# Down projection with weight sums made in HBM by transfers, seven products for sixteen groups

## The chip, the cores and the metric

One of the eight cores of a Trainium2 chip runs the kernel. The metric is the device time of one execution in microseconds. Engines: PE multiplies (TensorE), DVE and ACT (VectorE and ScalarE) work on vectors, POOL is GpSimd, SP only issues transfers. Matrix products of float32 data are made here in three passes: an operand is split into a high part (`hi`, type float32r) and the rest (`lo`), and high x high, low x high and high x low are added up in PSUM.

## The reference

A block of a language model on x of 256 rows by 2048, all in float32: normalization, a wide input projection, three kinds of attention, gates, an output projection, and a gated feed-forward part. The down projection at its end is what the change touches:

```python
def reference(x, mem, g_mix, w_in, ...):
    ...
        g = jax.nn.sigmoid(gates.reshape(b, s, N_BRANCH, D_MODEL) + b_gate[l])
        merged = (g[:, :, 0] * (o_fox @ w_br_fox[l])
                  + g[:, :, 1] * (o_sb @ w_br_sb[l])
                  + g[:, :, 2] * (o_mem @ w_br_mem[l]))
        x = x + merged @ w_out[l]

        h2 = rms_norm(x, g_ffn[l])
        u = causal_depthwise_conv(h2 @ w_up[l], conv_w[l], conv_b[l])
        u_gate, u_val = jnp.split(u, 2, axis=-1)
        x = x + (jax.nn.silu(u_gate) * u_val) @ w_down[l]
    return x
```

`w_down` has 5632 rows and 2048 columns.

## The kernel before, in words

The stages follow each other: memory keys and values, attention projections with the heads between them, gates and branch products (`w_in`, `w_br_*`; from about 301 us), output projection (`w_out`, first load at 658.6 us), up projection (`w_up`, first load at 748.4 us) and down projection (`w_down`, first load at 1239.7 us).

**Weights.** Everywhere a weight tile of 128 partitions by 1024 float32 (512 KB) is loaded by SP into a ring of four buffers (tag `raw`, `WBUFS` = 4), ACT casts it to `hi` and DVE subtracts to get `lo` (rings of four each, `SBUFS`). In the stages ahead of the down projection that is `piece` (L135 to L137), in the down projection `load` (L785) and `parts` (L792, L793). A raw buffer is free for the next load when its last reader, mostly the DVE subtraction, is done.

**Background work.** `later` puts a generator in a queue; `tick()`, called once after each weight piece (and twice in each group of the down projection), advances up to two of them by one step. `finish()` ticks until none is left. The order of instructions on an engine is then settled by the framework's scheduler, which takes what is ready by priority; DMAs on one issuing engine start in its order, and `keep_in_program_order` holds an instruction to its place.

**Down projection.** The 44 tiles of rows of `w_down` are taken in 22 groups of two, once for each half of the columns (`nb` = 0, 1; `n0` = 0, 1024). Y and X are four PSUM banks each. A letter of `plans` says how a group is made:

- `e`, function `eight`: eight products of 128x128 by 128x512 (two row tiles of the input, two column pieces, two row tiles of weights), three matmuls each: 24 matmuls, two loads.
- `s`, function `seven`: a scheme of Strassen's kind for the group's 2x2 blocks: seven products, 21 matmuls. It needs sums of weight blocks, B01 and B11 being the second halves of the two raw tiles: T1 = B00 + B01, T3 = B11 + B01 (`t13`), T2 = T1 + B11, T4 = T2 + B10 (`t24`), made on DVE (L828, L829, L832, L833), and sums of the input's blocks, made once for each group by `forms` (L774 to L781) and kept in `sf` for both halves (eight places). `gather` adds Y's banks into the residual after the last `s`.

`forms` is called behind an eight while sevens are left in this half. `sums` gives a DVE scratch tile from a ring of two.

In `plans` before, the first half has 5 sevens and 17 eights, the second 7 and 15. At the end of a half, four adds (L893) and transfers (L894, issued by ACT) bring the result out. No transfer is issued by POOL.

Of the kernel before, what the change touches and what calls it, by code (L numbers as in the profile page):

```python
# [9 lines left out]
F32 = mybir.dt.float32  # L10
F32R = mybir.dt.float32r
AF = mybir.ActivationFunctionType
ALU = mybir.AluOpType
AX = mybir.AxisListType

P = 128
# [16 lines left out]
PIECE = 1024  # L33
# [8 lines left out]
def hybrid_block(  # L42
# [25 lines left out]
    nc = tc.nc  # L68
# [3 lines left out]
    wp = ctx.enter_context(tc.tile_pool(name="wp", bufs=WBUFS))  # L72
# [8 lines left out]
    def bank(name):  # L81
        return pp.tile([P, 512], F32, tag="bank", name=name)
# [14 lines left out]
    def later(gen):  # L97
        waiting.append(gen)

    def tick():  # L100
        while waiting and len(active) < WINDOW:
            active.append([waiting.popleft(), 0])
        for a in list(active):
            if a[1] > 0:
                a[1] -= 1
                continue
            try:
                a[1] = next(a[0]) or 0
            except StopIteration:
                active.remove(a)  # L110
# [7 lines left out]
    def finish():  # L118
        while waiting or active:
            tick()  # L120

    pinned = [True]

# [181 lines left out]
    def block(name, dt=F32):  # L305
        return bp.tile([P, 1024], dt, tag="blk", name=name)
# [4 lines left out]
    def rows_of(b):  # L311
        return b.rearrange("p (t n) -> p t n", t=NT)
# [72 lines left out]
    transposed(memT, memres, gmem, 2, "mT")  # L385
    kv_part(0, 1, wh1[:, 0], wl1[:, 0])
    tick()
    xT = None
    for k in range(1, KT):
# [52 lines left out]

    ps = proj(C_MQ, MEM_W, "mq")
    finish()
    qm = heads_of(block("qm"))
    y = norm_heads(ps, rstd, "mq")
# [164 lines left out]
        later(sb_head(h))  # L611


    mT = [None] * (KT // 2)
    branches = ((w_br_fox, 0, N_FOX, 0), (w_br_mem, N_FOX + N_SB, N_MEM, 2), (w_br_sb, N_FOX, N_SB, 1))

    def merged_T(acc, n):
        yield 2
        for pr in range(2):
            m = block(f"mT_{n}_{pr}", F32R).rearrange("p (j s) -> p j s", j=2)  # L620
            tp = bank(f"mt_{n}_{pr}")
            for j in range(2):
                for t in range(NT):
                    c = (2 * pr + j) * P
                    nc.tensor.transpose(tp[:, j * S + t * P : j * S + (t + 1) * P], acc[:, t, c : c + P], ident)
            for j in range(2):
                split_to(m[:, j], tp[:, j * S : (j + 1) * S])
            mT[2 * n + pr] = m
            yield

    for n in range(4):
        n0 = n * 512
        gate = []
        for b in range(3):
            bg = gp.tile([P, 512], F32, tag="bg", name=f"bg_{n}_{b}")
            nc.sync.dma_start(bg, b_gate[0, b, n0 : n0 + 512].partition_broadcast(P))
            ps = proj(C_GATE + b * D + n0, 512, f"g{n}_{b}")
            g = rows_of(block(f"g_{n}_{b}"))
            for t in range(NT):
                nc.vector.scalar_tensor_tensor(g[:, t], ps[t], rstd[:, t : t + 1], bg, ALU.mult, ALU.add)  # L640
            if n > 0:
                nc.scalar.activation(g, g, AF.Sigmoid)
            gate.append(g)
        if n == 0:
            finish()
            for g in gate:
                nc.scalar.activation(g, g, AF.Sigmoid)
        acc = rows_of(block(f"acc_{n}"))
        for i, (w, k0, nk, b) in enumerate(branches):
            ps = product(lambda k: oT[:, k0 + k], w[0], nk, n0, 512, f"b{n}_{b}")  # L650
            for t in range(NT):
                g = gate[b]
                if i == 0:
                    nc.vector.tensor_tensor(acc[:, t], g[:, t], ps[t], ALU.mult)
                else:
                    nc.vector.tensor_tensor(g[:, t], g[:, t], ps[t], ALU.mult)
                    nc.vector.tensor_tensor(acc[:, t], acc[:, t], g[:, t], ALU.add)
        later(merged_T(acc, n))


    hT = xt_pool.tile([P, KT, 2 * S], F32R, tag="xt", name="hT")
# [67 lines left out]
    for f0 in range(0, FT, 4):  # L729
        for s in range(2):  # L730
            ps = [bank(f"u{f0 + i}_{s}") for i in range(4)]
            c0 = s * D_FF + f0 * P
            for k in range(0, KT, 2):
                hi, lo = piece(upv[:, k : k + 2, c0 : c0 + 512], 2, 512, f"u{f0}_{s}_{k}")
                for j in range(2):
                    first, last = k + j == 0, k + j == KT - 1
# [18 lines left out]
    def sums(name):  # L755

        if not dn:
            uv.close()
            dn.append(ctx.enter_context(tc.tile_pool(name="dn", bufs=2)))
        return dn[0].tile([P, 1024], F32, tag="ts", name=name)  # L760

    ov = out[0].rearrange("(t p) d -> p t d", p=P)
    dv = w_down[0].rearrange("(k p) n -> p k n", p=P)
    FS3, FS1, FS2, FS4 = range(4)
    sf = xt_pool.tile([P, 8, 4, 2, P], F32R, tag="xt", name="sf")

# [16 lines left out]
    def load(k, n0):  # L783
        raw = wp.tile([P, PIECE], F32, tag="raw", name=f"raw_d{n0}_{k}")
        nc.sync.dma_start(raw, dv[:, k, n0 : n0 + PIECE])  # L785
        return raw

    def parts(src, name):
        n = src.shape[1]
        hi = wp.tile([P, PIECE], F32R, tag="hi", bufs=SBUFS, name=f"hi_{name}")  # L790
        lo = wp.tile([P, PIECE], F32R, tag="lo", bufs=SBUFS, name=f"lo_{name}")
        nc.scalar.copy(hi[:, :n], src)  # L792
        nc.vector.tensor_tensor(lo[:, :n], src, hi[:, :n].bitcast(F32), ALU.subtract)  # L793
        return [(hi[:, i : i + 512], lo[:, i : i + 512]) for i in range(0, n, 512)]

    def three(o, ah, al, w, first=False, last=False):
        nc.tensor.matmul(o, lhsT=ah, rhs=w[0], start=first, stop=False)  # L797
        nc.tensor.matmul(o, lhsT=al, rhs=w[0], start=False, stop=False)  # L798
        nc.tensor.matmul(o, lhsT=ah, rhs=w[1], start=False, stop=last)  # L799

    def a_of(k, t):
        return aT[:, k, t * P : (t + 1) * P], aT[:, k, S + t * P : S + (t + 1) * P]

    def f_of(p, f):
        return sf[:, p, f, 0], sf[:, p, f, 1]
# [15 lines left out]

    def seven(p, n0, X, Y, first, last):
        k0, k1 = 2 * p, 2 * p + 1
        raw0, raw1 = load(k0, n0), load(k1, n0)
        t13 = sums(f"t13_{n0}_{p}")
        t24 = sums(f"t24_{n0}_{p}")
        b01, b11 = raw0[:, 512:], raw1[:, 512:]
        nc.vector.tensor_tensor(t13[:, :512], raw0[:, :512], b01, ALU.add)  # L828
        nc.vector.tensor_tensor(t13[:, 512:], b11, b01, ALU.add)  # L829
        (B00,) = parts(raw0[:, :512], f"d{n0}_{k0}")  # L830
        three(Y[0], *a_of(k0, 0), B00, first, last)
        nc.vector.tensor_tensor(t24[:, :512], t13[:, :512], b11, ALU.add)  # L832
        nc.vector.tensor_tensor(t24[:, 512:], t24[:, :512], raw1[:, :512], ALU.add)  # L833
        B10, B11 = parts(raw1, f"d{n0}_{k1}")
        three(X[0][0], *a_of(k1, 0), B10)
        three(X[0][1], *f_of(p, FS4), B11)
        tick()
        T1, T3 = parts(t13, f"t13_{n0}_{p}")
        three(Y[2], *f_of(p, FS1), T1, first, last)
        three(Y[3], *f_of(p, FS3), T3, first, last)  # L840
        T2, T4 = parts(t24, f"t24_{n0}_{p}")
        three(Y[1], *f_of(p, FS2), T2, first, last)
        three(X[1][0], *a_of(k1, 1), T4)
        tick()

# [16 lines left out]
        nc.vector.tensor_tensor(xr(1, 0), xr(1, 0), f[:, :512], ALU.add)  # L862
        nc.vector.tensor_tensor(xr(1, 1), xr(1, 1), f[:, 512:], ALU.subtract)

    plans = ("eeee" + "see" * 5 + "eee", "eee" + "se" * 7 + "eeeee")
    formed = 0
    for nb, plan in enumerate(plans):
        n0 = nb * PIECE
        Y = [bank(f"y{nb}_{i}") for i in range(4)]
        X = [[bank(f"x{nb}_{t}_{n}") for n in range(2)] for t in range(NT)]  # L870
        ns, s, e = plan.count("s"), 0, plan.count("s")
        for i, c in enumerate(plan):
            if c == "s":
                seven(s, n0, X, Y, s == 0, s == ns - 1)
                s += 1
                if s == ns:
                    later(gather(n0, Y))
            else:
                eight(e, n0, X, i == 0, i == len(plan) - 1)
                e += 1  # L880
                if e >= 2 and s < ns and formed <= (s if nb == 0 else ns - 1):
                    forms(formed)
                    formed += 1
        finish()
        for t in range(NT):
            for n in range(2):
                o = sm.tile([P, 512], F32, tag="junk", bufs=2, name=f"o_{nb}_{t}_{n}")
                parts_ = 2 if (nb, t, n) == (1, 1, 1) else 1
                for i in range(parts_):
                    w = 512 // parts_  # L890
                    oc = slice(i * w, (i + 1) * w)
                    xc = slice(n0 + n * 512 + i * w, n0 + n * 512 + (i + 1) * w)
                    nc.vector.tensor_tensor(o[:, oc], xres[:, t, xc], X[t][n][:, oc], ALU.add)  # L893
                    nc.scalar.dma_start(ov[:, t, xc], o[:, oc])  # L894
# [31 lines left out]
```

## Time and profile before

| what | value |
|---|---|
| median of 3 runs | 1498.74 us (1497.72 to 1501.03) |
| span of the profiled execution, first to last instruction | 1494.4 us |
| median less span | 4.3 us |
| granted TensorE clock, mean | 1.000 |
| PE busy | 1483.2 us, 99% |
| DVE, ACT, POOL busy | 1014.0, 794.0, 16.1 us |
| DMA over the span | 283.62 MB, mean 190 GB/s |
| read from HBM, written to HBM | 280.23 MB, 2.10 MB |
| loads of `raw_d` | 88, each 512 KB, median 4.7 us from issue to landing |

How to read it: times in a trace count from the first instruction; those given as results are of whole executions, which are some 4 us longer than the span. A row of a window gives the busy time of each engine in that stretch and, behind an x, how many instructions it had. The DMA share is the mean busy share of the core's 16 DMA engines. A group's row gives its line, engine, operation, tiles and shapes, count, busy time and mean ns of one, then the engine's idle time just before, and what ended it. Matmul records last 0.39 us and overlap, so the time that one takes is read from start to start.

### The profile page before, as it was taken

The page shows a single profiled execution, that of the slowest core. Times are in us where ns is not written, and L with a number is a line of the kernel's source. Part 1 is how long each engine was busy: PE and PEld are TensorE (multiplying, and loading weights), DVE is VectorE, ACT ScalarE, POOL GpSimd, SP SyncE. Part 2 cuts the span into 40 slices and gives each one's busy share as a digit, 9 for nine tenths or more (in the row PEclk, how much of TensorE's full clock was granted, in tenths as well). Part 3 has the DMA queues.
Part 4 walks back from the last instruction along what each step waited for, and adds up shares of the span by engine and source line. Part 5 has one row for each costly group of instructions (what it writes and reads, how often), then busy time and mean ns, then how long its engine had stood idle before and what let it go on. Part 6 is the DMA issues. An engine that isn't in the chain of part 4 may idle for free.

```text
span 1494.4 us, 19871 instructions
## 1 busy us (share of the span) xinstructions
PE 1483.2 (99%) x7429; PEld 1255.9 (84%) x7429; DVE 1014.0 (68%) x1465; ACT 794.0 (53%) x1108; POOL 16.1 (1%) x46
## 2 busy tenths in 40 slices
PE   8999999999999999999999999999999999999998
PEld 6888888888888888888888888888888888888777
DVE  5767566555655646555557778777778778987885
ACT  6755454358544444444456556556556656553552
POOL 0000000001000000000000000000000000000000
PEclk9999999999999999999999999999999999999999
DMA  8665475365666666655555665655656565556554
GB/s 291 193 211 158 126 220 167 119 211 164 188 194 210 185 210 203 185 190 190 184 182 183 198 191 184 196 190 184 198 187 191 186 196 183 199 188 228 185 202 140
DMA packets 138543, 283.62 MB, mean 190 GB/s; under 512 B 9275, under 2 KB 18127, under 8 KB 138447
## 3 DMA queue, kind: packets, MB, share of 16 engines
q1 hardware_dynamic: 137118, 280.26, 59.0%
q10 hardware_dynamic: 1328, 2.11, 0.4%
q8 instruction: 58, 0.95, 0.2%
q14 instruction: 39, 0.31, 0.1%
HBM read 280.23 MB, written 2.10 MB: 189 GB/s over the span
## 4 chain that ended last, share of the span: by engine, by line
PE 95%; DMA 2%; ACT 1%; DVE 1%; issue 0%; POOL 0%; SPq 0%; DVEq 0%; POOLq 0%; ACTq 0%
PE u L739 21%; PE u L740 11%; PE g L147 5%; PE g L148 5%; PE g L149 5%; PE x L797 4%; PE x L798 4%; PE x L799 4%; PE s L147 2%; PE s L149 2%; PE f L147 2%; PE f L149 2%; PE s L148 2%; PE f L148 2%; PE o L147 2%; PE o L149 2%
## 5 line engine op out<-in xcount | busy, mean ns | idle before, releaser
L739 PE MATMUL u<-hT,hi_u 128*128 128x512 f32 x1408 | 488.5, 392 | 0.0
L740 PE MATMUL u<-hT,lo_u 128*128 128x256 f32 x1408 | 395.1, 281 | 0.0
L739 PEld LDWEIGHTS u<-hT,hi_u 128*128 128x128 f32 x1408 | 263.3, 187 | 57.3
L137 DVE TENSOR_TENSOR lo_u<-raw_u,hi_u 128x1024 fp32r<-128x1024 f32 x176 | 215.4, 1224 | 116.0 <-ACT hi_u L136 115.9
L740 PEld LDWEIGHTS u<-hT,lo_u 128*128 128x128 f32 x1408 | 266.8, 189 | 0.0
L136 ACT CAST hi_u<-raw_u 128x1024 fp32r<-128x1024 f32 x176 | 184.7, 1050 | 138.4 <-PE u L739 106.5
L137 DVE TENSOR_TENSOR lo_g<-raw_g,hi_g 128x1024 fp32r<-128x1024 f32 x96 | 117.7, 1229 | 101.3 <-ACT hi_g L136 98.8
L136 ACT CAST hi_g<-raw_g 128x1024 fp32r<-128x1024 f32 x96 | 100.7, 1051 | 121.8 <-PE g L148 97.4
L147 PE MATMUL g<-hi_g,xT 128*128 128x512 f32 x384 | 151.1, 393 | 0.0
L149 PE MATMUL g<-lo_g,xT 128*128 128x512 f32 x384 | 149.8, 390 | 0.0
L148 PE MATMUL g<-hi_g,xT 128*128 128x512 f32 x384 | 149.7, 390 | 0.0
L792 ACT CAST hi_d<-raw_d 128x1024 fp32r<-128x1024 f32 (+1 forms) x88 | 86.7, 993 | 74.6 <-PE x L798 38.7
L793 DVE TENSOR_TENSOR lo_d<-raw_d,hi_d 128x1024 fp32r<-128x1024 f32 (+1 forms) x88 | 99.8, 1148 | 16.2 <-ACT hi_d L792 16.2
L797 PE MATMUL x<-hi_d,aT 128*128 128x512 f32 x268 | 104.4, 390 | 0.0
L799 PE MATMUL x<-lo_d,aT 128*128 128x512 f32 x268 | 104.4, 390 | 0.0
L798 PE MATMUL x<-hi_d,aT 128*128 128x512 f32 x268 | 104.4, 390 | 0.0
L149 PEld LDWEIGHTS g<-lo_g,xT 128*128 128x128 f32 x384 | 72.1, 188 | 15.2
L148 PEld LDWEIGHTS g<-hi_g,xT 128*128 128x128 f32 x384 | 72.2, 188 | 14.5
L147 PEld LDWEIGHTS g<-hi_g,xT 128*128 128x128 f32 x384 | 72.2, 188 | 14.6
L137 DVE TENSOR_TENSOR lo_s<-raw_s,hi_s 128x1024 fp32r<-128x1024 f32 (+1 forms) x40 | 44.7, 1118 | 37.2 <-ACT hi_s L136 37.2
L137 DVE TENSOR_TENSOR lo_f<-raw_f,hi_f 128x1024 fp32r<-128x1024 f32 (+1 forms) x40 | 44.7, 1120 | 34.5 <-ACT hi_f L136 33.0
L136 ACT CAST hi_f<-raw_f 128x1024 fp32r<-128x1024 f32 (+1 forms) x40 | 38.5, 966 | 52.5 <-PE f L148 47.6
(318 smaller groups left out, 2554.3 us busy)
## 6 DMA issues: line engine op xcount, KB each, us to landing
raw_u<-in_w_up_dram SPq DMA_DIRECT2D x176, 512.0 KB, 4.0
raw_g<-in_w_in_dram SPq DMA_DIRECT2D x96, 512.0 KB, 3.6
raw_d<-in_w_down_dram SPq DMA_DIRECT2D x88, 512.0 KB, 4.7
raw_f<-in_w_in_dram SPq DMA_DIRECT2D x32, 512.0 KB, 3.5
raw_s<-in_w_in_dram SPq DMA_DIRECT2D x32, 512.0 KB, 3.4
raw_o<-in_w_out_dram SPq DMA_DIRECT2D x32, 512.0 KB, 4.7
raw_kv<-in_w_mem_kv_dram SPq DMA_DIRECT2D x15, 512.0 KB, 5.4
raw_b<-in_w_br_fox_dram SPq DMA_DIRECT2D x12, 512.0 KB, 4.0
```

What stands on the lines that cost most here:

```text
L136: pin(nc.scalar.copy(hi[:, :m], raw[:, :m]))
L137: pin(nc.vector.tensor_tensor(lo[:, :m], raw[:, :m], hi[:, :m].bitcast(F32), ALU.subtract))
L147: nc.tensor.matmul(o, lhsT=xh, rhs=wh, start=first, stop=False)
L148: nc.tensor.matmul(o, lhsT=xl, rhs=wh, start=False, stop=False)
L149: nc.tensor.matmul(o, lhsT=xh, rhs=wl, start=False, stop=last)
L739: nc.tensor.matmul(ps[i], lhsT=hi[:, j, c], rhs=hT[:, k + j, :], start=first, stop=False)
L740: nc.tensor.matmul(ps[i][:, :S], lhsT=lo[:, j, c], rhs=hT[:, k + j, :S], start=False, stop=last)
L792: nc.scalar.copy(hi[:, :n], src)
L793: nc.vector.tensor_tensor(lo[:, :n], src, hi[:, :n].bitcast(F32), ALU.subtract)
L797: nc.tensor.matmul(o, lhsT=ah, rhs=w[0], start=first, stop=False)
L798: nc.tensor.matmul(o, lhsT=al, rhs=w[0], start=False, stop=False)
L799: nc.tensor.matmul(o, lhsT=ah, rhs=w[1], start=False, stop=last)
```

## The change

After the first column of gates, generators for 16 groups' weight sums (eight for each half of the columns) are put in a second queue, `slow`. `aside()`, called at each tick, advances the first of them by one step at every fourth call. Each has four steps: ACT issues a transfer from HBM to HBM that copies B01 to four places of a 1 MB tile there; then POOL issues three transfers that add: B00 to the first three places, B11 to the last three, B10 to the third. The places then hold T1, T2, T4, T3. A fifth call ends the generator.

`seven` no longer adds on DVE. It loads the first half of its first raw tile, its second raw tile, and the four sums as two tiles, all through the ring of four raw buffers, and splits them as before; the order of products is a little different. Both halves of the columns have 8 sevens and 14 eights, in the same plan, and `forms` may run one group further ahead.

```diff
     def tick():
+        aside()
         while waiting and len(active) < WINDOW:
...
+    slow, pace = deque(), [0]
+
+    def aside():
+        pace[0] += 1
+        if slow and pace[0] % 4 == 0:
+            try:
+                next(slow[0])
+            except StopIteration:
+                slow.popleft()
...
+    dram = ctx.enter_context(tc.tile_pool(name="dram", bufs=1, space=bass.MemoryType.DRAM))
+    dv = w_down[0].rearrange("(k p) n -> p k n", p=P)
+    made = {}
+
+    def weight_sums(p, n0):
+        B = lambda j, n: dv[:, 2 * p + j : 2 * p + j + 1, n0 + n * 512 : n0 + (n + 1) * 512]
+        T = dram.tile([P, 4, 512], F32, name=f"sums_{n0}_{p}")
+        tc.keep_in_program_order(nc.scalar.dma_start(T, B(0, 1).to_broadcast([P, 4, 512])))
+        yield
+        nc.gpsimd.dma_start(T[:, :3], B(0, 0).to_broadcast([P, 3, 512]), accum_op=ALU.add)
+        yield
+        nc.gpsimd.dma_start(T[:, 1:], B(1, 1).to_broadcast([P, 3, 512]), accum_op=ALU.add)
+        yield
+        nc.gpsimd.dma_start(T[:, 2:3], B(1, 0), accum_op=ALU.add)
+        made[n0, p] = T
+        yield
...
         later(merged_T(acc, n))
+        if n == 0:
+            for nb, count in enumerate((8, 8)):
+                for p in range(count):
+                    slow.append(weight_sums(p, nb * PIECE))
...
     def seven(p, n0, X, Y, first, last):
         k0, k1 = 2 * p, 2 * p + 1
-        raw0, raw1 = load(k0, n0), load(k1, n0)
-        t13 = sums(f"t13_{n0}_{p}")
-        t24 = sums(f"t24_{n0}_{p}")
-        b01, b11 = raw0[:, 512:], raw1[:, 512:]
-        nc.vector.tensor_tensor(t13[:, :512], raw0[:, :512], b01, ALU.add)
-        nc.vector.tensor_tensor(t13[:, 512:], b11, b01, ALU.add)
+        raw0 = wp.tile([P, PIECE], F32, tag="raw", name=f"raw_d{n0}_{k0}")
+        nc.sync.dma_start(raw0[:, :512], dv[:, k0, n0 : n0 + 512])
+        raw1 = load(k1, n0)
+        T = made[n0, p].rearrange("p f n -> p (f n)")
+        ts = []
+        for i in range(2):
+            t = wp.tile([P, PIECE], F32, tag="raw", name=f"raw_t{i}_{n0}_{p}")
+            nc.sync.dma_start(t, T[:, i * PIECE : (i + 1) * PIECE])
+            ts.append(t)
         (B00,) = parts(raw0[:, :512], f"d{n0}_{k0}")
         three(Y[0], *a_of(k0, 0), B00, first, last)
-        nc.vector.tensor_tensor(t24[:, :512], t13[:, :512], b11, ALU.add)
-        nc.vector.tensor_tensor(t24[:, 512:], t24[:, :512], raw1[:, :512], ALU.add)
         B10, B11 = parts(raw1, f"d{n0}_{k1}")
         three(X[0][0], *a_of(k1, 0), B10)
         three(X[0][1], *f_of(p, FS4), B11)
         tick()
-        T1, T3 = parts(t13, f"t13_{n0}_{p}")
+        T1, T2 = parts(ts[0], f"t12_{n0}_{p}")
         three(Y[2], *f_of(p, FS1), T1, first, last)
+        three(Y[1], *f_of(p, FS2), T2, first, last)
+        T4, T3 = parts(ts[1], f"t43_{n0}_{p}")
         three(Y[3], *f_of(p, FS3), T3, first, last)
-        T2, T4 = parts(t24, f"t24_{n0}_{p}")
-        three(Y[1], *f_of(p, FS2), T2, first, last)
         three(X[1][0], *a_of(k1, 1), T4)
         tick()
...
-    plans = ("eeee" + "see" * 5 + "eee", "eee" + "se" * 7 + "eeeee")
+    plans = ("eee" + "se" * 8 + "eee", "eee" + "se" * 8 + "eee")
...
-                if e >= 2 and s < ns and formed <= (s if nb == 0 else ns - 1):
+                if e >= 2 and s < ns and formed < 8 and formed <= s + 1:
                     forms(formed)
                     formed += 1
```

More of the change, by code (lines that the diff above doesn't have):

```diff
@@ L762, in hybrid_block @@
     ov = out[0].rearrange("(t p) d -> p t d", p=P)
-    dv = w_down[0].rearrange("(k p) n -> p k n", p=P)
     FS3, FS1, FS2, FS4 = range(4)
```

## The prediction

> **What bounds the kernel now.** I read the page's first two parts, then the windows by stage, then the groups and tiles of the down projection (from 1255 us), then who waited for whom.
>
> ```profile
> PE 1483.2 (99%) x7429; PEld 1255.9 (84%) x7429; DVE 1014.0 (68%) x1465; ACT 794.0 (53%) x1108; POOL 16.1 (1%) x46
> ...
> q1 hardware_dynamic: 137118, 280.26, 59.0%
> ```
> ```profile
> core 0: us, PE busy (x) PEld busy (x) DVE busy (x) ACT busy (x) POOL busy (x), PEclk, DMA share, GB/s
> 20.00:40.00 20.00, 19.41 (x92) 15.25 (x91) 13.98 (x28) 17.16 (x36) 0.00 (x0) 1.00 0.99 351
> 400.00:660.00 260.00, 260.00 (x1160) 215.31 (x1159) 149.14 (x154) 113.08 (x116) 0.00 (x0) 1.00 0.64 197
> 660.00:750.00 90.00, 90.00 (x415) 74.78 (x414) 54.16 (x61) 40.59 (x54) 0.00 (x0) 1.00 0.57 187
> 750.00:1240.00 490.00, 490.00 (x2810) 431.59 (x2809) 367.01 (x607) 290.61 (x447) 0.00 (x0) 1.00 0.60 189
> 1272.00:1370.00 98.00, 98.00 (x434) 81.23 (x433) 87.52 (x123) 50.74 (x55) 0.00 (x0) 1.00 0.60 200
> ...
> 1385.00:1460.00 75.00, 72.85 (x318) 58.98 (x317) 62.83 (x72) 41.19 (x44) 0.00 (x0) 1.00 0.58 195
> ```
>
> PE is busy 260 of 260, 90 of 90 and 490 of 490 us in the gates, the output projection and the up projection, at the full granted clock: a matmul that goes is time that goes, one for one. The DMA engines are about 0.6 busy there; their ceiling, seen from 20 to 40 us, is 351 GB/s at a share of 0.99.
>
> The price of a matmul in the down projection is its start-to-start time, not the 0.39 us that a record lasts:
>
> ```profile
> 1267.61 0.39 PE L797 MATMUL x<-hi_d,aT 128*128 128x512 f32 x1
> ...
> 1270.33 0.39 PE L797 MATMUL x<-hi_d,aT 128*128 128x512 f32 x1
> ...
> 1270.70 0.43 DVE L774 TENSOR_TENSOR fw<-aT 128x256 f32<-128x256 f32 x1
> ...
> 1272.82 0.69 DVE L828 TENSOR_TENSOR t<-raw_d 128x512 f32<-128x512 f32 x1
> ...
> 1274.04 0.68 DVE L781 TENSOR_TENSOR sf<-fr,sf 128x512 fp32r<-128x512 f32 x1
> ```
>
> The two PE rows are twelve matmuls apart (four groups of three): 2.72 us, 0.227 us each. An eight is 24 of them (5.45 us), a seven 21 (4.77 us). In the second column half, where sevens alternate with single eights, PE loses time: 75 us should hold 332 records at the 98 us row's pace (434 in 98) and hold 318, so 14 x 0.227 = 3.2 us are lost. Who ended those waits:
>
> ```profile
> PE y L799 <- DVE lo_t L793: 2.2, 2, 1.4
> ```
> ```profile
> 1385.61 0.69 DVE t L833
> 1386.30 1.15 DVE lo_d L793
> 1387.46 4.04 DMA raw_d<-in_w_down_dram
> 1392.13 1.23 DVE lo_t L793
> ```
>
> That is the chain load, add, split, matmul: an add (L833) and a split hold a raw buffer, its reload takes 4 us, and the next split of a sum comes too late.
>
> **The change, part by part.**
>
> *Matmuls.* Before, the plans hold 5 + 7 = 12 sevens in 44 groups; after, 8 + 8 = 16. Four eights become sevens: 4 x 3 = 12 matmuls, 12 x 0.227 = -2.7 us, all of it on the path.
>
> *Adds.* Twelve sevens lose four DVE adds each.
>
> ```profile
> L793 DVE TENSOR_TENSOR lo_d<-raw_d,hi_d 128x1024 fp32r<-128x1024 f32 x73 | 87.9, 1221 | 10.4 <-ACT hi_d L792 10.4
> L792 ACT CAST hi_d<-raw_d 128x1024 fp32r<-128x1024 f32 x73 | 76.0, 1052 | 55.0 <-PE x L798 35.3 <-DMA raw_d<-in_w_down_dram 6.9 <-issue 4.1
> ...
> L793 DVE TENSOR_TENSOR lo_d<-raw_d,hi_d 128x512 fp32r<-128x512 f32 x12 | 8.3, 688 | 1.1 <-ACT hi_d L792 1.1
> L833 DVE TENSOR_TENSOR t<-t,raw_d 128x512 f32<-128x512 f32 x12 | 8.3, 688 | 0.1
> ```
>
> That is 12 x 4 x 0.69 = 33 us of DVE, off the path except for the 3.2 us of PE waits: those end with a split that stood behind an add, so I count -3.2 us. Four more sevens bring 4 x 1.5 more splits (7 us), and an eighth call of `forms`. In the first half all eight forms now fall: a seven and an eight need five splits and a half (6.1 + 0.7 us) and one form, which by the rows above takes 1270.70 to 1272.82 plus 0.68, 2.8 us: 9.6 of 10.2 us. That is tight, but before, a seven with two eights was as tight: four adds 2.8, seven splits 8.5, a half 0.7, a form 2.8, 14.8 of 15.7 us, and from 1272 to 1370 no PE time was lost. I count 0 for it.
>
> *The start.*
>
> ```profile
> L797 PE MATMUL x<-hi_d,aT x268: 387/390/398, 1255.3 to 1489.2; 128*128 128x512 f32 x134
> ```
>
> With "eee" ahead instead of "eeee", PE reaches the first seven 72 matmuls after 1255.3 us, at 1271.7, and its form FS4 six matmuls later, at 1273.0. The form's low part (L781) started at 1274.04 behind two adds of 0.6 us each that are gone; without them it ends near 1274.1. About +1 us.
>
> *Loads in the down stage.* A seven loaded 1.05 MB; now it loads half a tile, one tile and two tiles of sums: 1.84 MB. A seven and an eight move 2.88 MB in 10.2 us, 283 GB/s, where 195 to 200 flowed. The ceiling is 351, so bandwidth suffices; but only four raw buffers exist, six tiles go through them per 10.2 us, and each is held from issue to the end of its split.
>
> ```profile
> DMA to landing us min/median/max: 3.5/4.7/6.4
> ```
> ```profile
> DMA to landing us min/median/max: 4.2/5.4/8.3
> ```
>
> The first row is raw_d's in the down stage, the second raw_kv's, at the start, near the ceiling. A loop is landing + cast 1.05 + split 1.22 + 0.2 of handing on (an estimate); six tiles through four buffers take 1.5 loops, less 0.43 us for the half tile (half its load at 351 GB/s 0.75, cast 0.43 and split 0.53, shared by four). At 4.7 us: 1.5 x 7.17 - 0.43 = 10.33 us, 0.11 over the 10.22 of a seven and an eight, so 16 x 0.11 = +1.7 us. At 3.5 us: 0. At 5.4 us: 11.38, 16 x 1.16 = +18.5 us. I take the median of these very loads, 4.7: the demand of 283 lies between the two rows' rates, but loads would come 1.7 us apart and not in bunches behind adds.
>
> *Making the sums.* From about 400 us (32 ticks of 2.7 us for each of three gate columns, ahead of 660) `aside` takes one step in four ticks, a sum in 20 ticks, 54 us. Each sum is a 1.05 MB copy issued by ACT and adds of 0.79, 0.79 and 0.26 MB issued by POOL. ACT: 16 issues at 0.34 us (below) = 5 us, on an engine 47% idle whose casts mostly wait for PE. A copy waits for nothing but a completion counter; the casts of the next pieces queue behind it, and they run up to four pieces (10 us) ahead of PE. POOL: its last real work is the stick-breaking masks; behind its adds stand only more adds. SP gets 32 more issues at 0.33 us in 231 us; its loads of sums wait for adds that landed long before.
>
> ```profile
> L785 SPq DMA_DIRECT2D raw_d<-in_w_down_dram x88: 327/328/432, 1239.7 to 1470.4; - x88
> ```
> ```profile
> L894 ACTq DMA_DIRECT2D out_dram<-o x9: 338/339/444, 1369.2 to 1491.5; - x9
> ```
>
> The 16 sums write 16.8 MB by copying and 29.4 MB by adding within some 850 us. At the price of a load (280 MB for 59.0% of 1494 us, 318 GB/s at full share) that is 145 us, 17 points on a share of 0.60: 0.77, no room problem. No row shows an adding transfer, so its price has bounds: a load (1), and above, whatever fills the engines: (16.8 + 29.4c)/318 reaches the free 0.40 x 850 = 340 us at c = 3.1. Below 1 nothing is won, since loads aren't late there:
>
> ```profile
>   ACT hi_u L136: 115.9, 112
>   PE u L739: 106.5, 93
>   issue: 16.4, 11
> ```
>
> These are what ended the idle time of the engines that split raw_u: no DMA among them. A load that comes some 5 us late is covered by raw and split buffers. I take 2, midway: (16.8 + 58.8)/318 = 238 us, 28 points, a share of 0.88, and 0 us on PE.
>
> The Trainium skill ("Collectives: The Full Stack", the part on the bandwidth ceiling) says that an adding transfer needs two source reads where a copy needs one, and so reaches half its rate; by that rule the price is 2, which no run here shows, and the sum would stay as it is; the speed is the engines', not the adder's. It also says ("DMA: Bandwidth & Descriptors", "Issuing engines are not separate DMA queues") that transfers of all issuers share the same 16 engines; no run shows two big queues at once yet.
>
> **Sum.** -2.7 - 3.2 + 1.0 + 1.7 + 0 = -3.2 us. The profiled execution spans 1494.4 us; the median of the runs is 1498.74, 4.3 more, which lies outside the span and isn't touched. So 1491.2 in the span, 1495.5 timed.
>
> **Rivals.**
>
> *Hidden gain eaten, no change:* landing of 4.8 to 4.9 us in the down stage (16 x 0.26 = 4.2 to 16 x 0.41 = 6.6 us), or a few gate or up pieces late by as much. Against the -4.9 of the other terms: 1498 to 1500.4. For it: the forecast's loop has no slack at all.
>
> *The four raw buffers take over from the adds (slower).* Place: sevens and eights in the down stage; point: landing above 4.95 us; price at raw_kv's 5.4: -4.9 + 18.5, so 1512.3. For it: 283 GB/s is nearer to 351 than the present 200. Against it: at 200 GB/s and in bunches the median was still 4.7 us.
>
> *The DMA engines fill up from the gates on (slower).* Point: an adding transfer dearer than 3.1 loads. At 3.5: (16.8 + 102.9)/318 = 376 us, 36 over the 340, so 1498.7 - 4.9 + 36 = about 1530. Against it: a share of 0.60 to start from.
>
> *It doesn't do what it says:* sums finished too late, sevens waiting on SP. The last of 16 is asked for near 1450 us, 66 us for each from 400 on; it needs the saturation above, so it counts little.
>
> **How the numbers follow.** A run tells about 0.2% (3 us) from no change. Forecast 0.42 (1493 to 1495.7), no change 0.18, four buffers 0.25, engines full 0.13, too late 0.02: faster 0.42, same 0.18, slower 0.40. The range runs from 1492.5 (neither the start's wait nor the loop's: 1498.7 - 5.9 = 1492.8) to 1513 (the dearer loop); the saturated cases and a few others, under 0.2, lie outside. The forecast's own range is 1492.5 to 1495.7.
>
> **What would show it.** Right: 1008 matmuls in the down stage, L797 to L799 336 each; no adds of raw tiles on DVE; PE whole from 1280 on; raw and sum loads landing within 4.7 us; DMA share 0.75 to 0.9 from 400 us on, with PE still at 260 of 260 and 490 of 490. Wrong: casts in the down stage idle behind DMA for tens of us and PE under 98%, with landings above 5 us (four buffers); or gate and up casts that wait for raw_g and raw_u (engines full); or sevens waiting for a sum.

## The result, and the profile after

| | before | after |
|---|---|---|
| median of the runs | 1498.99 us (4 runs, 1497.72 to 1501.03) | 1540.47 us (4 runs, 1534.46 to 1544.26) |
| ratio of the times, 95% interval | | 1.0273 [1.0248, 1.0299]: slower by 41.5 us |
| span of the profiled execution | 1494.4 us | 1536.9 us (its time 1538.67) |

The time of an execution is 1.8 us more than its own span here; the 4.3 us that the prediction added are the median of before against the span of one execution.

The prediction was 1495.5 us in a range of 1492.5 to 1513. It was wrong in its sign, and the time lies outside the range.

The first and third parts of the page after:

```profile
PE 1500.6 (98%) x7417; PEld 1254.0 (82%) x7417; DVE 992.5 (65%) x1432; ACT 794.1 (52%) x1117; POOL 69.5 (5%) x94
...
q1 hardware_dynamic: 141726, 292.84, 58.3%
q0 software_dynamic: 15104, 29.36, 15.6%
q10 hardware_dynamic: 9776, 18.88, 5.9%
```

PE has twelve matmuls fewer, as it should, and DVE is 21 us lighter. New are q0 (POOL's adding transfers) and the bytes of q10 (ACT's copies, beside 2.11 MB that were there before). Two columns give the price of a MB in time of the DMA engines: share x 16 x 1536.9 us / MB. A load costs 49 us, a copy 77 and an adding transfer 131. So a copied MB costs 1.6 loads and an added one 2.7, with all of them at work together.

The windows by stage after (gates, output projection, up projection, and the first half of the down projection):

```profile
core 0: us, PE busy (x) PEld busy (x) DVE busy (x) ACT busy (x) POOL busy (x), PEclk, DMA share, GB/s
400.00:660.00 260.00, 259.70 (x1157) 214.64 (x1156) 146.73 (x153) 108.46 (x114) 15.93 (x14) 1.00 0.94 245
660.00:750.00 90.00, 88.51 (x400) 72.42 (x399) 54.50 (x61) 40.33 (x53) 4.18 (x4) 1.00 0.91 237
750.00:1240.00 490.00, 477.68 (x2686) 413.49 (x2685) 340.24 (x563) 268.11 (x417) 27.89 (x25) 1.00 0.88 229
...
1272.00:1370.00 98.00, 90.11 (x387) 71.07 (x386) 77.61 (x125) 50.73 (x64) 3.33 (x3) 0.97 0.81 242
```

The DMA share rose to 0.88 to 0.94, where 0.88 was forecast. But PE is no longer whole: 477.68 of 490 us in the up projection with 2686 records where 2810 were. Where the 42 us went is read from the first matmul of each stage in the two traces. From gates to output projection: 365.6 us before, 367.7 after. Output projection: 90.7 and 91.6. Up projection: 489.3 and 514.3. First to last matmul of the down projection: 234.4 and 250.2. These make 44 us; the stages ahead of the gates took 1.4 us less. So 25 of the 42 us were lost in the **up projection**, ahead of everything that uses the sums, and 16 in the down projection, where time was to be won.

Why, the DMA view and the waits say. First the landing times after (the last column is the median in us), then before:

```profile
raw_u<-in_w_up_dram SPq DMA_DIRECT2D x176, 512.0 KB, 7.0
raw_g<-in_w_in_dram SPq DMA_DIRECT2D x96, 512.0 KB, 5.3
raw_d<-in_w_down_dram SPq DMA_DIRECT2D x72, 512.0 KB, 5.5
sums<-in_w_down_dram POOLq DMA_DIRECT2D x32, 768.0 KB, 12.8
...
sums<-in_w_down_dram ACTq DMA_DIRECT2D x16, 1024.0 KB, 12.6
raw_o<-in_w_out_dram SPq DMA_DIRECT2D x32, 512.0 KB, 8.7
...
sums<-in_w_down_dram POOLq DMA_DIRECT2D x16, 256.0 KB, 6.0
```
```profile
raw_u<-in_w_up_dram SPq DMA_DIRECT2D x176, 512.0 KB, 4.0
raw_g<-in_w_in_dram SPq DMA_DIRECT2D x96, 512.0 KB, 3.6
```

The loads of the output projection (`raw_o`, 4.7 us before) came later still than `raw_u`, and yet that stage lost only 0.9 us: how late a load comes doesn't alone tell what it costs. The spread of raw_u, after and then before, and who waited after:

```profile
DMA to landing us min/median/max: 3.8/7.0/11.8
```
```profile
DMA to landing us min/median/max: 3.3/4.0/4.6
```
```profile
ACT hi_u L147 <- DMA raw_u<-in_w_up_dram: 113.5, 51, 9.1
...
ACT hi_g L147 <- DMA raw_g<-in_w_in_dram: 59.3, 27, 6.9
...
PE u L772 <- DVE lo_u L148: 11.3, 14, 2.0
PE y L830 <- DVE lo_t L824: 6.4, 13, 1.0
```

ACT's casts, none of whose waits in the up projection ended with a DMA before, now wait 51 times for `raw_u`, up to 9.1 us. A part comes through to PE as waits for the low split. The transfers of one sum (1 + 0.75 + 0.75 + 0.25 MB) are under way for about 12.6 + 12.8 + 12.8 + 6.0 = 44 of the 57 us between two sums (15 intervals from 409.7 to 1271.0 us), so most loads fall beside one of them.

### The profile page after: what moved, and what is told of

It reads as the page before. It is cut to its first block, busy times and chain, and to the rows that moved or that the text cites. A ratio compares the mean times of both kernels' runs of the same rounds, so it can differ in the third digit from the quotient of the medians.

```text
span 1536.9 us, 19992 instructions
## 1 busy us (share of the span) xinstructions
PE 1500.6 (98%) x7417; PEld 1254.0 (82%) x7417; DVE 992.5 (65%) x1432; ACT 794.1 (52%) x1117; POOL 69.5 (5%) x94
## 3 DMA queue, kind: packets, MB, share of 16 engines
q0 software_dynamic: 15104, 29.36, 15.6%
## 4 chain that ended last, share of the span: by engine, by line
PE 53%; DMA 27%; DVE 11%; ACT 6%; issue 2%; POOL 0%; SPq 0%; ACTq 0%; DVEq 0%; POOLq 0%
DMA raw_u<-in_w_up_dram 12%; PE u L771 8%; DMA raw_d<-in_w_down_dram 6%; PE u L772 4%; PE g L158 4%; PE g L160 4%; PE g L159 4%; DVE lo_u L148 3%; DMA raw_g<-in_w_in_dram 3%; DMA raw_t<-sums 2%; PE s L158 2%; PE s L160 2%; PE f L158 2%; PE s L159 2%; PE f L159 2%; PE f L160 2%
## 5 line engine op out<-in xcount | busy, mean ns | idle before, releaser
L771 PE MATMUL u<-hT,hi_u 128*128 128x512 f32 x1408 | 494.5, 395 | 2.8 <-ACT hi_u L147 2.8
L147 ACT CAST hi_u<-raw_u 128x1024 fp32r<-128x1024 f32 x176 | 182.7, 1048 | 162.1 <-DMA raw_u<-in_w_up_dram 113.5
L830 PE MATMUL x<-lo_d,aT 128*128 128x512 f32 x240 | 93.8, 391 | 1.0 <-DVE lo_d L824 1.0
L828 PE MATMUL x<-hi_d,aT 128*128 128x512 f32 x240 | 93.7, 390 | 0.0
L829 PE MATMUL x<-hi_d,aT 128*128 128x512 f32 x240 | 93.4, 389 | 0.0
## 6 DMA issues: line engine op xcount, KB each, us to landing
sums<-in_w_down_dram POOLq DMA_DIRECT2D x32, 768.0 KB, 12.8
sums<-in_w_down_dram ACTq DMA_DIRECT2D x16, 1024.0 KB, 12.6
```

The lines of the kernel that those rows point to most:

```text
L147: pin(nc.scalar.copy(hi[:, :m], raw[:, :m]))
L771: nc.tensor.matmul(ps[i], lhsT=hi[:, j, c], rhs=hT[:, k + j, :], start=first, stop=False)
```

## The experiments

Two theories stood first. *Making* (A in the expectations): the transfers that make the sums slow the loads of the stages that they run beside. *Using* (B in the expectations): the sevens' six tiles through four raw buffers, a rival of the prediction. Two more came with the result of the stages: that DVE's work in the up projection turns late loads into PE waits (E), or that the transfers cost wherever they run (D; in e4's expectation D is that the mean share decides, in e7's that the amount does). Each kernel was timed beside the kernel before on its own chip (medians 1498.02, 1496.87 and 1496.44 us in the three sets).

### Making alone, using alone

**e1_make_only**: the sums are made as in the change; `seven`, `plans` and the condition of `forms` are those of before, so that nobody reads the sums. Its edit against the change:

```diff
-        T1, T2 = parts(ts[0], f"t12_{n0}_{p}")
+        T1, T3 = parts(t13, f"t13_{n0}_{p}")
...
-    plans = ("eee" + "se" * 8 + "eee", "eee" + "se" * 8 + "eee")
+    plans = ("eeee" + "see" * 5 + "eee", "eee" + "se" * 7 + "eeeee")
```

> The sums are made in HBM as in the changed kernel, but nothing reads them: the down projection is that of the kernel before (12 sevens, adds on DVE). Theory A, loads come late while a sum's transfers are under way: the loss of the changed kernel between 400 and 1280 us stays whole, gates +2, output projection +1, up projection +25 us, and the down stage is within 3 us of before: about 1525 us. Rival, the loss in the up projection comes with the changed plan or order of the down stage (another schedule) and not with the transfers: under 1503 us.

Measured: 1534.51 us, ratio 1.0241 [1.0223, 1.0258], so +36.5 us, where about 26 were expected (1525). In the profiled execution, the slowest of the five (1546.55), the up projection takes 520.5 us and the down projection 248.9, 15 more than before, where 3 at most were expected: the last transfer landed only at 1326 us. So making costs time in the down projection too, though nobody uses the sums there.

**e2_use_only**: the sevens of the change, but no sums are made; two tiles of `w_down` are loaded in their place.

```diff
-            nc.sync.dma_start(t, T[:, i * PIECE : (i + 1) * PIECE])
+            nc.sync.dma_start(t, dv[:, k0 + i, n0 : n0 + PIECE])
```

> No sums are made; each seven loads two tiles of w_down in the place of the two tiles of sums (same sizes and ring, so part of the output is computed from other numbers). Theory B, six tiles through four raw buffers in 10.2 us: gates to up as before (489 us for the up projection), landings in the down stage above 5 us, PE waits of 0.7 to 1.2 us for each seven, in all 12 to 16 us more than the 228.5 us that 1008 matmuls take: 1505 to 1510 us. Rival C, the down stage lost its time to transfers still running until 1310 us: no waits here, 1493 to 1496 us.

Measured: 1503.84 us, 1.0036 [1.0021, 1.0051], +5.8 us. 1505 to 1510 was expected; the down projection takes 240.7 us, 12 more than its matmuls need, as expected. The two together make 42.3 us, the change 41.5: the medians add up, and both theories hold, 6 to 1. Using costs 5.8 us instead of winning 3.2 as in the sum. Its largest wait of PE in the down projection, then its landings:

```profile
PE y L826 <- DVE lo_t L820: 6.2, 12, 0.8
```
```profile
raw_d<-in_w_down_dram SPq DMA_DIRECT2D x72, 512.0 KB, 5.1
...
raw_t<-in_w_down_dram SPq DMA_DIRECT2D x32, 512.0 KB, 5.8
```

Landing is 5.1 to 5.8 us, past the 4.95 from which the four buffers were to decide.

### What of making costs: adding, pace, DVE, bursts

**e3_plain**: e1 without the adding; the same bytes are written by plain transfers from POOL (the tiles then hold no sums; nobody reads them).

```diff
-        nc.gpsimd.dma_start(T[:, :3], B(0, 0).to_broadcast([P, 3, 512]), accum_op=ALU.add)
+        nc.gpsimd.dma_start(T[:, :3], B(0, 0).to_broadcast([P, 3, 512]))
```

> As e1_make_only, but the three transfers of POOL copy where they added (the sums are wrong, and nobody reads them): same bytes written, no second read. Theory A with the price of an adding packet as its cause (254 ns for 2 KB against 101 of a load and about 150 of a copy, worked out from the page of the changed kernel): the share of the engines falls by some 8 points, each transfer lands in 8 us where it took 12.8, and the up projection loses under 10 us: 1502 to 1508 us. Rival, it is the number of transfers or their issue by POOL that costs: 1518 us and more.

Measured: 1511.0 us, 1.0094 [1.0078, 1.0109], +13.0 us. It is 3 us more than the theory had at most and 7 less than the rival. Of e1's 36.5 us, 23.5 are due to the adding. POOL's queue in the page's third part, then the landings:

```profile
q0 software_dynamic: 7936, 29.36, 9.7%
```
```profile
raw_u<-in_w_up_dram SPq DMA_DIRECT2D x176, 512.0 KB, 5.6
...
sums<-in_w_down_dram POOLq DMA_DIRECT2D x32, 768.0 KB, 9.9
```

A MB costs 9.7% x 16 x 1508.2 / 29.36 = 80 us when copied from POOL, as from ACT, against 131 when added: adding is 1.6 copies, and a copy 1.6 loads. The Trainium skill ("Collectives: The Full Stack", the part on the bandwidth ceiling) has adding at half the rate of a copy, since it reads two sources. By the traces it is a little better against a copy (1.6), but 2.7 against a load into the chip's memory, which was the unit of the sum.

**e4_half**: e1 with 8 sums instead of 16 and half the pace.

```diff
-        if slow and pace[0] % 4 == 0:
+        if slow and pace[0] % 8 == 0:
...
-            for nb, count in enumerate((8, 8)):
+            for nb, count in enumerate((4, 4)):
```

> As e1_make_only, but eight sums and a step at every eighth call, so half the transfers over the same time; each sum's four transfers still follow each other at once. Theory A in its burst form, each sum costs what it costs while under way: half the loss, 13 us: about 1512 us. Rival D, the average share of the engines decides (0.75 here, 0.9 in the changed kernel): the loss is gone, under 1502 us.

Measured: 1517.52 us, 1.013 [1.0102, 1.0158], +19.5 us, 2.4 us for a sum, against 36.5/16 = 2.3 in e1. The window of the up projection in e4:

```profile
750.00:1240.00 490.00, 482.75 (x2738) 420.48 (x2737) 353.20 (x587) 279.18 (x430) 15.79 (x14) 1.00 0.77 211
```

The cost halves with the sums; it doesn't vanish at a share of 0.77. So making is **not free when the mean share leaves room**: at 0.77 a sum costs what it costs at 0.88.

**e5_light**: e1 without two of the three multiply-adds of the convolution on DVE (part of the computation is left out).

```diff
-        nc.vector.scalar_tensor_tensor(y, u[:, 1 : S + 1], tap(1), y, ALU.mult, ALU.add)
-        nc.vector.scalar_tensor_tensor(y, u[:, 0:S], tap(0), y, ALU.mult, ALU.add)
```

> As e1_make_only, but the convolution after the up projection leaves out its two tap operations on DVE (so the output is another one), which takes about 0.8 of 2.2 us of DVE for each of 88 calls, some 70 us of 367 in the up projection. Question: why the up projection lost 25 to 31 us to the transfers and the gates, with the engines as full, only 2 to 4. Theory E, a load that comes late can't be made up there because DVE also has the convolution to do: the up projection falls from 514 to 520 us to 500 or less. Rival F, DVE has nothing to do with it (loads land later there, 7.0 against 5.3 us, by where the weights lie): it stays at 510 or more.

It asks why the gates lost 2 us at a share of 0.94 and the up projection 25 at 0.88. The theory: in the up projection DVE also has the convolution, in a settled order; a split whose load came late stands behind it and can't catch up. Measured: 1512.98 us in two runs, 1.0114 [1.008, 1.0149]. The window in e5:

```profile
750.00:1240.00 490.00, 487.32 (x2750) 422.68 (x2748) 292.57 (x427) 274.20 (x429) 29.53 (x27) 1.00 0.89 235
```

The loads are as late as ever (raw_u 7.3 us), but PE is busy 487.3 of 490 us, and the up projection takes 501.2 us instead of 514 to 520, close to the 500 that was named. From 750 to 1240 us the gaps between its matmuls (start to start, over their usual distance) sum to 4.7 us instead of e1's 20.2. That supports the theory. It shows that DVE's load turns late loads into PE waits; that the fixed order is what does it, and not the amount of work, was not separated. The rival, that loads land later there, has the output projection against it, whose loads landed later still.

**e7_spaced**: 8 sums, those of the second half, in 8 ticks a step; POOL's transfers wait for a marker of ACT's, so that each starts at its own tick and none follows another closely.

```diff
+    def add(dst, src, name):
+        m = sm.tile([P, 2], F32, tag="mark", bufs=2, name=f"mark_{name}")
+        tc.keep_in_program_order(nc.scalar.copy(m[:, :1], qscale))
+        tc.keep_in_program_order(nc.gpsimd.tensor_copy(m[:, 1:], m[:, :1]))
+        tc.keep_in_program_order(nc.gpsimd.dma_start(dst, src, accum_op=ALU.add))
```

> As e4_half (eight sums, read by nobody), but each adding transfer is held back by a tiny POOL copy that waits for a mark written by ACT at its own step, so that the four transfers of a sum start some 22 us apart and never follow each other at once. Same bytes, same average share as e4_half, 1517.5 us. Theory A in its burst form, the raw buffers run dry only in 40 us and more of transfers without a break: no waits of PE on late splits in the up projection, within 3 us of before (1498). Rival D, it is the amount that counts: 1512 us or more.

Measured: 1526.44 us, 1.0207 [1.019, 1.0223], +29.6 us: more than e4 with the same bytes. The theory that only transfers in close succession cost fell: these start 23 us apart on average and take 12 to land. Why they cost more than e4's isn't settled. The sums are also made in less time (the last lands at 1144 us, e4's at 1253), and the markers are new work on ACT and POOL. POOL's issue of a 256 KB add at 1041.5 us, 9 us after the add before it had landed, and what follows on ACT, DVE and PE:

```profile
1041.49 0.85 POOL L645 DMA_DIRECT2D sums<-in_w_down_dram  x1
...
1051.59 1.05 ACT L147 CAST hi_u<-raw_u 128x1024 fp32r<-128x1024 f32 x1 [7.06 <-DMA raw_u<-in_w_up_dram]
...
1055.15 1.22 DVE L148 TENSOR_TENSOR lo_u<-raw_u,hi_u 128x1024 fp32r<-128x1024 f32 x1
1056.28 0.87 DVE L754 SCALAR_TENSOR_TENSOR y<-u,taps,y 128x256 f32<-128x256 f32 x2
...
1057.87 0.75 DVE L761 TENSOR_TENSOR y<-y,y 128x256 f32<-128x256 f32 x2
1058.54 0.41 DVE L749 TENSOR_TENSOR cr<-cr,u 128x256 f32<-128x256 f32 x1
...
1061.48 0.39 PE L777 MATMUL u<-hT,lo_u 128*128 128x256 f32 x1 [1.61 <-DVE lo_u L148]
```

The load issued at 1043.7 us landed 10.4 us later; for the one ahead of it ACT waited 7.06 us; then DVE, which had run dry, did its splits one by one with the convolution's steps between them (L749 to L761, those of 1056.28 to 1058.9 in a row), and the next split came late for PE by 1.6 us. This fits e5's theory in one instance. Counted by queue and microsecond in the same trace, the loads moved 43 to 107 GB/s while this add ran (1043 to 1048 us), where the stage needs about 190. While the 1 MB copy issued at 1064.2 us ran, they moved 0 to 16 GB/s for five microseconds (1067 to 1072) and the copy 92 to 258. The Trainium skill ("DMA: Bandwidth & Descriptors", "Queues, rings and completion order") says that an engine takes queues in turn, packet by packet. An even turn is not what these rows show: the copy had the engines nearly alone. Why, no run here settles.

### Using with another buffer

**e6_halfbuf**: e2 with a buffer of its own (2 KB a partition) for the half tile, so that five tiles instead of six go through the four buffers in a seven and an eight.

```diff
-        raw0 = wp.tile([P, PIECE], F32, tag="raw", name=f"raw_d{n0}_{k0}")
+        raw0 = dn[0].tile([P, 512], F32, tag="r0", bufs=1, name=f"raw_d{n0}_{k0}")
```

> As e2_use_only, with one edit: the half tile of a seven has a buffer of its own, so five tiles and not six go through the four raw buffers in a seven and an eight. Theory B: 1.25 loops of 5.5 + 2.5 us are 10.0 us, under 10.2, so the down stage falls from 240.7 us to 230 to 233 and the whole to about 1495. Rival, the DMA engines can't deliver 283 GB/s here: the stage stays at 240 and the whole at 1503.

Measured: 1492.79 us, 0.9975 [0.9965, 0.9984], -4.1 us against before, where e2 had +5.8: one buffer is worth 9 to 10 us. The same wait line as above, and the window from 1255 us in e2 and then in e6:

```profile
PE y L826 <- DVE lo_t L820: 1.0, 2, 0.5
```
```profile
1255.00:1372.00 117.00, 113.67 (x490) 90.60 (x489) 98.05 (x146) 66.28 (x78) 0.00 (x0) 1.00 0.73 242
```
```profile
1255.00:1372.00 117.00, 115.34 (x501) 93.03 (x500) 98.08 (x145) 65.45 (x78) 0.00 (x0) 1.00 0.77 253
```

More GB/s (253 against 242), a landing about as late (5.1 and 5.5 us), and the waits go from 6.2 to 1.0 us: it was the count of buffers and not the bandwidth.

**e8_change_halfbuf**: the whole change with this one edit.

> The changed kernel whole, with the edit of e6_halfbuf alone (a buffer of its own for the half tile). If the two costs add, making the sums 36 us and using them 6 (e1_make_only, e2_use_only), the edit takes 9 to 11 us off the changed kernel's 1540: about 1530. If the loss in the down stage is by now that of the last transfers and not of the four buffers, 1538 or more.

Measured: 1534.37 us, 1.0248 [1.0226, 1.0271], against the change's 1.0273: about 4 us better by the ratios, whose intervals overlap; by the whole time a gain of 9 to 10 us isn't shown. In the profiled executions the down projection takes 239.2 us instead of 250.2, but e8's is its lowest (1528.17 of 1528.17 to 1537.62 us). The gaps of PE in it tell more: up to 1323 us they make 9.4 us in e8 (5.5 of them at one wait at 1298 us) and 8.1 in the change, after that 1.3 and 13.2. So the buffer takes away what e2 had (11.8 us of gaps), and what is left stands where the last sums are still being made, up to about 1315 us (rival C of e2's expectation, true in part). The groups of `sums` in the change show it (first and last start):

```profile
L862 SPq DMA_DIRECT2D raw_t<-sums x32: 326/327/330, 1292.0 to 1501.4; - x32
...
L638 POOL DMA_DIRECT2D sums<-in_w_down_dram x16: 852/852/876, 447.5 to 1309.4; - x16
```

### Making elsewhere

**c1_second_half**: first half as before; second half with 8 sevens that use the sums and the extra buffer; the 8 sums made as in e7.

```diff
-    plans = ("eee" + "se" * 8 + "eee", "eee" + "se" * 8 + "eee")
+    plans = ("eeee" + "see" * 5 + "eee", "eee" + "se" * 8 + "eee")
...
-                seven(s, n0, X, Y, s == 0, s == ns - 1)
+                (seven_t if nb else seven)(s, n0, X, Y, s == 0, s == ns - 1)
```

> A version that could beat both: first half of the columns as before (5 sevens, adds on DVE), second half with 8 sevens from eight spaced sums as in e7_spaced, the half tile in a buffer of its own. If e7_spaced is free and e6_halfbuf holds, it saves one group's three matmuls (0.7 us) and the 3.1 us that PE waits in the second half before: about 1495 us. If the amount of transfers counts, 1510 us or more; if the four buffers still bind, about 1500.

Measured: 1522.45 us, 1.0177 [1.016, 1.0195]. It missed what was hoped, since spacing the transfers doesn't free them: against e7 on the same chip it is 4.0 us faster (their intervals just overlap), about the gain of using in e6; the rest is e7's cost.

**c2_gates_only**: c1 with a step every 3 ticks (c1 has 8, the change 4) and no markers, so that all 8 sums are made in gates and output projection, where e5's theory had lateness covered.

```diff
-        if slow and pace[0] % 4 == 0:
+        if slow and pace[0] % 3 == 0:
```

> As c1_second_half, without spacing, a step at every third call: all eight sums are made in the gates and the output projection and none in the up projection. Theory E, in those stages DVE has time to make up a late load and in the up projection it hasn't: up projection back at 489 us, gates and output projection 3 to 6 us longer, down stage 231 us: 1496 to 1500. Rival D, each transfer costs what it costs wherever it runs: about 1515, as c1_second_half did.

Measured: 1541.64 us, 1.0302 [1.0288, 1.0316]. The windows of gates and up projection, then the landing of the gates' loads:

```profile
400.00:660.00 260.00, 236.36 (x994) 186.81 (x992) 125.14 (x133) 93.19 (x98) 21.36 (x19) 0.97 0.96 236
...
750.00:1240.00 490.00, 490.00 (x2756) 428.81 (x2755) 355.59 (x570) 284.93 (x435) 0.00 (x0) 1.00 0.60 189
```
```profile
raw_g<-in_w_in_dram SPq DMA_DIRECT2D x96, 512.0 KB, 9.6
```

Expected were 1496 to 1500 by E and about 1515 by D, and both missed by far. The up projection is whole again (489.3 us), so nothing but the transfers beside it had slowed it. The down projection has no gap at all: 230.3 us for 1017 matmuls, so the sevens of the change cost nothing once their sums are made in time and the half tile has its own buffer. But the gates grew from 365.6 to 415.8 us. Here the engines were full in earnest: 8 sums take, by this run's packets, 8 x 20.3 us of all engines, and the loads of the 272 us that this stretch lasted before take 0.64 x 272 = 174; together 336 us, and it took 320 (404 to 724). So the gates bear lateness only while the engines have gaps; neither E, by which this should have cost 3 to 6 us, nor D, by which the gates of the change should have lost more than 2 us, is the whole of it.

### The plan alone

**b1_plan**: the kernel before, with the second half's sevens spread as the first half's are, and one seven fewer. Nothing of the change is in it.

```diff
-    plans = ("eeee" + "see" * 5 + "eee", "eee" + "se" * 7 + "eeeee")
+    plans = ("eeee" + "see" * 5 + "eee", "ee" + "see" * 6 + "ee")
```

> The kernel before with one edit: the plan of the second half is "ee" + "see" * 6 + "ee", so six sevens two eights apart as in the first half, where seven stood one eight apart. No sums in HBM. If the 3.1 us that PE waits in the second half come from sevens standing too close for the adds, they go, and three matmuls come back (+0.7): 2.4 us faster, 0.16%. Rival: the waits move with the sevens: the same or 0.7 slower.

Measured: 1492.08 us (8 runs, 1491.70 to 1492.95), 0.9969 [0.9958, 0.9979]. It beats both kernels. It has three matmuls more than before and no PE gap in the down projection:

```profile
1255.00:1372.00 117.00, 117.00 (x518) 96.89 (x517) 100.51 (x146) 60.64 (x72) 0.00 (x0) 1.00 0.61 201
```

The down projection takes 231.7 us for 234.4 before, the 2.4 us that were expected and a little more; what made the rest of the 4.4 the traces don't show. The waits behind DVE's adds, which the change takes away with the adds, go by another order of the groups.

## Why the prediction was wrong, point by point

- **Matmuls, -2.7 us: right.** 1008 records at 0.2267 us are 228.5 us, and the down projection takes that plus its gaps (e6: 228.5 + 3.6 = 232.1, 232.2 measured; the change: 228.5 + 21.3 = 249.8, 250.2 measured). Only e7 and c1 ran at another pace (last section).
- **Waits behind DVE's adds, -3.2 us: right in size.** b1 shows the 3.1 us of gaps gone once sevens stand two eights apart. In the change PE waits for the splits of sums instead (6.4 us), whose casts wait for their loads; in c2, with the buffer added, these are gone as well.
- **The start, +1.0 us:** in the change PE waited 0.8 us for the first form, close to it; in e6 its longest gap ahead of 1300 us is 0.4 us.
- **Loop through four raw buffers, +1.7 us: mis-sized.** The wait came where the formula had it, past its point of 4.95 us, but the landing put into it was wrong: 4.7 us was the median of before, 5.1 and 5.8 were measured in e2, where nothing else ran. The argument that loads 1.7 us apart would land no later was the failed step. Between e2 and e6 the one buffer is worth 9 to 10 us (their ratios differ by 0.0061, 9.2 us; the down projection went from 240.7 to 232.2). The formula is too dear as well: at 5.1 us it gives 16 x 0.7 = 11 us, at 5.8 28. The rival's 18.5 us was too dear, the forecast's 1.7 too cheap.
- **Making the sums, "0 us on PE": the step that failed,** with 36.5 us. Its arithmetic was off: the price of adding was taken as 2 loads and is 2.7, that of copying as 1 and is 1.6. By its own sum that is (16.8 x 1.6 + 29.4 x 2.7)/318 = 334 us of all engines and not 238, of the 340 that were free. But the missing room alone is not what failed: e4, with half the transfers, lost as much for each sum. What failed is the reading of a mean share as a cover: "a load that comes some 5 us late is covered by raw and split buffers". Loads came up to 11.8 us after their issue. Counted by microsecond between 760 and 1230 us, the loads moved less than 30 GB/s for up to 6 us at a stretch in the change, and likewise in e1, e4 and e7; before, for 3 at most.
- **The same cover was taken for two stages.** The gates had it, with DVE busy for 149 and ACT for 113 of 260 us (2.1 us lost). In the up projection DVE is busy 367 of 490 us before, the window that the prediction itself quoted, and there 25 us were lost; e5 takes the DVE work away and most of the loss with it.
- **The last sums were taken as done in time for the sevens,** and they were; but they were still being made until about 1315 us, beside the very stage that loads most. The prediction had 16 sums at 54 us from 400 on, which ends at 1264, and never asked what they do after 1255.
- **The rivals.** The nearest was "the DMA engines fill up from the gates on", with the signs that were named for it: casts of gates and up projection that wait for `raw_g` and `raw_u`. Its point, an adding price above 3.1, rests on copies at the price of a load; with 1.6 for these it would have been 2.8, and 2.7 was measured. So the change stood close to it. But it asked for engines with no room left, and the loss came in e4 at a share of 0.77 too; what full engines cost, c2 shows in the gates. "Four raw buffers take over" was true as well, at about half its price.

## What to carry to other kernels

Work given to idle DMA engines isn't free because their mean share leaves room: ask how long a transfer keeps a load from landing, set that against the lead that buffers give, and do it for the busiest stage that it runs beside. An adding transfer from HBM to HBM cost 2.7 times the engine time of a load of the same bytes here, and an engine with little slack behind the loads turns their lateness into time. Before moving work to another engine, see whether the wait goes by spacing the work out: here another order of groups in a plan won 4.4 us, and the change lost 41.5.

## What was not expected of the hardware

**The granted clock falls for short stretches after waits that are far from an idle engine.** Windows of the change around 960 and 1302 us:

```profile
955.00:960.50 5.50, 3.76 (x20) 2.79 (x19) 2.01 (x4) 2.54 (x4) 0.85 (x1) 1.00 0.98 304
960.50:963.90 3.40, 3.40 (x13) 2.81 (x12) 3.40 (x8) 2.56 (x5) 0.00 (x0) 0.50 0.78 188
1296.00:1301.80 5.80, 4.10 (x17) 2.82 (x16) 3.72 (x9) 2.66 (x4) 1.22 (x1) 1.00 0.90 318
1301.80:1308.70 6.90, 5.31 (x12) 3.84 (x13) 5.89 (x10) 2.25 (x3) 0.00 (x0) 0.51 1.01 249
```

PE was busy for some 70% of the 5.5 and 5.8 us ahead of them, and then had half the clock for 3.41 and 6.83 us, which costs at most half of that, about 5 us in all (an estimate). c2 had six such dips. The Trainium skill ("TensorE: Matmul & The Clock Gate", "What's actually happening") has a window of 3413 ns, which the lengths agree with; it speaks of an idle window, and no window here was idle throughout.

**Matmuls keep one of two rhythms.** In e3 the up projection lost 9.0 us with a single PE gap of 1.0 us, at 834.8 us. The high x 512-wide matmuls of that stage, counted in equal windows, before and in e3 (a wait at 834.8 lies between the first row and the second):

```profile
800.00:830.00 30.00, 30.00 (x88) 1.00 0.64 198
...
1000.00:1200.00 200.00, 200.00 (x578) 1.00 0.60 191
```
```profile
800.00:830.00 30.00, 30.00 (x88) 1.00 0.88 223
...
1000.00:1200.00 200.00, 200.00 (x567) 1.00 0.83 236
```

567 for 578 is 1.9% slower, for the remaining 427 us 8 us, though PE is busy throughout and the clock is 1.00. It isn't the traffic: c1's down projection, long after the last transfer, ran at 232.5 ns a matmul on average where b1's ran at 226.7, and without a gap. The like holds for e7, whose down projection began 133 us after the last transfer had landed and took 240.5 us with about the same gaps as before's 234.4 (3.4 and 3.1 us). In the change, gaps explain 22 of the 25 us of the up projection, and this the other 3. For long the slower rhythm stands only in runs that made sums beside the up projection. So a part of the price of making isn't late loads, and what sets the rhythm stays open.
